# Down-projection of a hybrid layer: sample columns in two transfers, samples and operand work behind the tile, another order of sums

## The chip, the cores and the metric

One core of a Trainium2 chip runs the whole program. The metric is the device time of one execution in microseconds. Engines and queues are named as in the profile: TensorE is PE (its weight loads PEld), VectorE is DVE, ScalarE is ACT, GpSimd is POOL, SyncE is SP. Every DMA of the stage concerned is issued by SP.

## The reference

One layer over 1024 prompt rows and 32 sample rows: a mixer (a state-space group and an attention group side by side), then a gated feed-forward. Width 1024, feed-forward width 2816. The change touches the last product:

```python
    x = x + jnp.concatenate([y_ssd, o], axis=-1) @ w_out
    f = rmsnorm(x, norm_ffn_g)
    x = x + (jax.nn.silu(f @ w_gate) * (f @ w_up)) @ w_down
```

It is taken for the prompt rows (1024 x 2816 by 2816 x 1024) and for the sample rows.

## The kernel before, in words

**Gate and up** come first (matmuls at L970, added up by DVE at L978). Their result, the activations of 22 blocks of 128 feed-forward columns, is formed block pair by block pair. For the prompt, `keep` (L1007) splits each of seven combinations per pair into a rounded part (ACT cast, L1012) and a remainder (DVE, L1013) and writes both to DRAM, `act_d` (L1015, 256 KB a write). It uses two sets of pieces of the tile `sc` in turn, so a combination waits for the writes of the one before the last. For the sample rows, a small slice per block goes to `asm_d` (L1003).

**Down** is lines 1036 to 1229. There are NP = 11 pairs `n` of weight blocks. A product of 2 x 2 blocks is made with seven products instead of eight; each product is three matmuls per pair (rounded by rounded, rounded by remainder, remainder by rounded). The work goes in six chunks, and in each over four token tiles `tp`:

```python
    chunks_ = [(0, 1)] + [(n, 2) for n in range(1, NP, 2)]
    tiles_ = [(n0, r, tp) for n0, r in chunks_ for tp in range(4)]
```

Chunk 0 has one pair (tiles of 21 matmuls), the others have two (42). `down_tile` (L1145) makes the seven products of a tile in banks `ps_z` and adds them into `Z` in SBUF (copies by ACT L1171 and DVE L1173 in chunk 0, additions by DVE L1160 later). The last chunk also combines and stores.

For each pair, `prep_down` (L1060) does four things: the **sample product** of 16 small matmuls (L1064) that wants the sample columns `asm` and both weight blocks `raw`; its addition to `x2s` (DVE, L1067); the **splits** of the operands into a rounded part (ACT, L1077) and a remainder (DVE, L1078); and the **sums** on POOL (L1082, L1083, L1085, L1086). The operands are W (one block, unsummed), X (the second `raw`), V (the first `raw` after two sums) and U (after two more). X, V and U take the next of nine slots in turn: five are pairs of tiles `whi`, `wlo`; four lie in `sd` (tag "lo"), in the memory of the `sc` pieces that `keep` wrote from.

Weight blocks come by `load_raw` (L1051, 512 KB each, two per pair), activations by `load_act` (L1045, 896 KB per pair and tile) into five slots: four in `fA` and `at5`. At the start of Down, SP issues `raw` of pairs 1 and 2, then `asm` in one transfer of 352 KB (L1127). A scheduler merges the order in which the code is written with what is ready; the built order below is its result. Per queue and engine, instructions run in that order.

Of the kernel before, what the change touches and what calls it, by code (L numbers as in the profile page):

```python
# [7 lines left out]
F32 = mybir.dt.float32  # L8
# [4 lines left out]
ALU = mybir.AluOpType  # L13
AX = mybir.AxisListType

P = 128
# [4 lines left out]
NS = 32  # L21
# [6 lines left out]
NF = 22  # L28
NP = NF // 2
# [14 lines left out]
def build(tc, a):  # L44
    nc = tc.nc
# [26 lines left out]
    def nm(s):  # L72
        cnt[0] += 1
        return f"{s}_{cnt[0]}"
# [43 lines left out]
    asm_d = dr.tile([P, NF, NS], F32, name="asm_d")  # L118
# [677 lines left out]
    units, _ = pipelined([unit(i, pair) for pair in range(4) for i in (ORDER if pair < 3 else LAST)] + [None, None])  # L796
# [108 lines left out]
    def wide():  # L905
        return pv.tile([P, 1024], F32, tag="w", bufs=4, name=nm("ps_w"))
# [7 lines left out]
    T2, T1, T3, B22, T4 = (tq.tile([P, 2, 4, H], F32R, name=n) for n in ("T2", "T1", "T3", "B22", "T4"))  # L914
# [13 lines left out]
    B11 = fA[:, :, 0:4, :]  # L928
    B21 = fA[:, :, 4:8, :]
# [102 lines left out]
    ats, raws, bops = {}, {}, {}  # L1032
# [4 lines left out]
    asm0 = mixS[:, 0:2, :]  # L1037
# [10 lines left out]
    def load_raw(n, pl, bufs):  # L1048
        raws[n] = [pl.tile([P, 1024], F32, tag="raw", bufs=bufs, name=nm("raw")) for _ in range(2)]
        for k in range(2):  # L1050
            nc.sync.dma_start(raws[n][k], a["wd"][2 * n + k])  # L1051

    def next_slot():
        k = b_turn[0]
        b_turn[0] += 1
        if k < 5:
            b_slots.append([wp.tile([P, 1024], F32R, tag=tag, bufs=5, name=nm(tag)) for tag in ("whi", "wlo")])
        return b_slots[k % 9]

    def prep_down(n, pb, act):  # L1060

        for k in range(2):
            for g in range(4):
                nc.tensor.matmul(pb[32 * g:32 * g + 32, 0:256], lhsT=act[:, k, :],  # L1064
                                 rhs=raws[n][k][:, g * 256:(g + 1) * 256], start=(k == 0), stop=(k == 1),
                                 tile_position=(0, 32 * g))
        nc.vector.tensor_tensor(x2s, pb[:, 0:256], x2s, op=ALU.add)  # L1067
        r1, r2 = raws.pop(n)
        b11, b12, b21, b22 = r1[:, 0:512], r1[:, 512:1024], r2[:, 0:512], r2[:, 512:1024]
        if n < 3:  # L1070
            c_slots.append(wp.tile([P, 1024], F32, tag="raw", bufs=3, name=nm("raw")))
        c = c_slots[n % 3].bitcast(F32R)
        W = [c[:, 0:512], c[:, 512:1024]]
        X, V, U = (next_slot() for _ in range(3))

        def split(t, src):
            nc.scalar.copy(out=t[0], in_=src)  # L1077
            nc.vector.tensor_tensor(t[1], src, t[0], op=ALU.subtract)  # L1078

        split(W, b11)  # L1080
        split(X, r2)
        nc.gpsimd.tensor_tensor(b12, b22, b12, op=ALU.subtract)  # L1082
        nc.gpsimd.tensor_tensor(b11, b12, b11, op=ALU.add)  # L1083
        split(V, r1)
        nc.gpsimd.tensor_tensor(b22, b22, b11, op=ALU.subtract)  # L1085
        nc.gpsimd.tensor_tensor(b21, b21, b11, op=ALU.subtract)  # L1086
        split(U, r2)
        op = lambda t, c: [x[:, c:c + 512] for x in t]
        bops[n] = dict(B11=op(W, 0), B21=op(X, 0), B22=op(X, 512), T2=op(V, 0), T3=op(V, 512), T4=op(U, 0), T1=op(U, 512))

    chunks_ = [(0, 1)] + [(n, 2) for n in range(1, NP, 2)]
    tiles_ = [(n0, r, tp) for n0, r in chunks_ for tp in range(4)]
# [3 lines left out]
    for k, (w, n) in enumerate(work):  # L1096
        end = k + 1 == len(work)
        cur = ops
        if not end:
            ops = prep(*work[k + 1])  # L1100
            use = use_up(n) if w else use_gate
        else:
            load_raw(0, wp, 3)
            nc.sync.dma_start(asm0, asm_d[:, 0:2])
            prep_down(0, wide(), asm0)

            def use(b, h, then=use_up(n)):
                if b == 0 and h == 0:
                    for m in range(4):
                        load_act(tiles_[m])  # L1110
                then(b, h)
        quad(cur, acts if w else gates, use)
        if w:
            keep_acts(n)
# [6 lines left out]
    pd = pool("pd", side="right")  # L1121
    pz = pool("pz", space=PSUM)
    Z = [pd.tile([P, 4, 512], F32, name=f"Z{k}") for k in range(7)]
    load_raw(1, pd, 4)
    load_raw(2, pd, 4)
    asm = pd.tile([P, NF, NS], F32, name="asm")
    nc.sync.dma_start(asm, asm_d)  # L1127
    at_slots.append(pd.tile([P, 7 * 2 * P], F32R, name="at5"))
    at_turn[0] = 4
    sd = hp.tile([P, KB * NT], F32R, tag="lo", name="sd")  # L1130
# [5 lines left out]
    def bank1():  # L1136
        return pz.tile([P, 512], F32, tag="z", bufs=8, name=nm("ps_z"))

    def residual(tp, rows, cols, z):
        x = pd.tile([P, 512], F32, tag="res", bufs=1, name=nm("res"))  # L1140
        r0 = 512 * rows + tp * P
        nc.sync.dma_start(x, xb_d[r0:r0 + P, 512 * cols:512 * cols + 512])
        nc.gpsimd.tensor_tensor(z, x, z, op=ALU.add)

    def down_tile(m):  # L1145
        n0, r, tp = tiles_[m]
        first, late, last = n0 == 0, n0 == NP - 4, n0 == NP - 2
        at = ats.pop(tiles_[m])
        z = [None] + [Z[i][:, tp, :] for i in range(7)]

        def product(q, name):
            pb = bank1()
            terms = [(k, x, y) for k in range(r) for x, y in ((0, 0), (0, 1), (1, 0))]
            for i, (k, x, y) in enumerate(terms):
                nc.tensor.matmul(pb, lhsT=at[k][:, q, x, :], rhs=bops[n0 + k][name][y], start=(i == 0),  # L1155
                                 stop=(i == len(terms) - 1))
            return pb

        def add(o, x, y, eng=nc.vector):
            eng.tensor_tensor(o, x, y, op=ALU.add)  # L1160

        def store(v, rows, cols):
            nc.sync.dma_start(a["o_yp"][(4 * rows + tp) * P:(4 * rows + tp + 1) * P, 512 * cols:512 * cols + 512], v)

        order = ((1, A11, "B11"), (6, S2, "T2"), (2, A12, "B21"), (5, S1, "T1"), (7, S3, "T3"), (3, S4, "B22"),
                 (4, A22, "T4"))
        if not last:
            for i, q, name in order:
                pb = product(q, name)
                if first and i in (1, 2, 5, 4):  # L1170
                    nc.scalar.copy(out=z[i], in_=pb)  # L1171
                elif first:
                    nc.vector.tensor_copy(z[i], pb)  # L1173
                else:
                    add(z[i], pb, z[i])
            if n0 in (3, 5):

                for i, rows, cols in ((2, 0, 0), (3, 0, 1), (4, 1, 0))[(0 if n0 == 3 else 2):(2 if n0 == 3 else 3)]:
                    residual(tp, rows, cols, z[i])
            if late:  # L1180

                add(z[6], z[1], z[6])
                add(z[2], z[1], z[2], nc.gpsimd)
                add(z[5], z[6], z[5])
                add(z[1], z[6], z[7])
                add(z[3], z[5], z[3], nc.gpsimd)
                add(z[7], z[5], z[7])
                add(z[4], z[1], z[4], nc.gpsimd)
                residual(tp, 1, 1, z[7])
            return  # L1190
        eng = nc.vector if tp == 3 else nc.gpsimd
        nc.scalar.copy(out=z[1], in_=product(A11, "B11"))
        add(z[6], product(S2, "T2"), z[1])
        add(z[2], z[1], z[2], eng)
        add(z[2], product(A12, "B21"), z[2])
        store(z[2], 0, 0)
        add(z[5], product(S1, "T1"), z[6])
        p7 = product(S3, "T3")
        add(z[7], z[5], z[7], eng)
        add(z[3], z[5], z[3], eng)  # L1200
        add(z[1], p7, z[6])
        add(z[7], p7, z[7])
        store(z[7], 1, 1)
        add(z[4], z[1], z[4], eng)
        add(z[3], product(S4, "B22"), z[3])
        store(z[3], 0, 1)
        add(z[4], product(A22, "T4"), z[4])
        store(z[4], 1, 0)

    def prep_next(n):  # L1210
        if n < NP:
            prep_down(n, bank1(), asm[:, 2 * n:2 * n + 2])
            if n + 2 < NP:
                load_raw(n + 2, pd, 4)

    for m in range(len(tiles_)):
        n0, r, tp = tiles_[m]

        if tp == (0 if r == 1 else 2):
            prep_next(n0 + r)  # L1220
        elif tp == 2:
            prep_next(n0 + r + 1)
        down_tile(m)
        if r == 2 and tp == 3:
            prep_next(n0 + r + 1)
        for k in {0: (4,), 2: (5,)}.get(m, (m + 2,) if m > 3 else ()):
            if k < len(tiles_):
                load_act(tiles_[k])
# [76 lines left out]
```

## Time and profile before

| | us |
|---|---|
| median of 3 runs | 1378.44 (1378.04 to 1383.52) |
| the profiled execution | 1378.53 |
| its span, first to last instruction | 1376.8 |
| TensorE busy | 1289.9 (94%) |
| DVE busy | 905.5 (66%) |
| POOL busy | 613.3 (45%) |
| ACT busy | 503.0 (37%) |

The span counts from the first to the last instruction; an execution's time is a little longer. Busy shares are means over stages of different kinds. The stage concerned begins at about 1122 us of the span, so it is the last 255 us. Times in the rows below count from the span's start.

### The profile page before, as it was taken

The numbers are of one execution on the slowest core, as the hardware profiler recorded it, in microseconds if no ns is written. First come the engines' busy times: TensorE is split into PE (matmuls) and PEld (weight loads), VectorE is DVE, ScalarE is ACT, GpSimd is POOL, SyncE is SP. The second block draws the span as 40 slices with busy tenths as digits, with TensorE's granted clock in tenths as the row PEclk, the third lists the DMA queues.
The fourth block names the chain that finished last, engine by engine and source line by source line (L and its number), as shares of the span: only waits on it lengthen the run. The fifth ranks groups of instructions, "written<-read, shape, count | busy, mean of one in ns | idle before, by whom it ended". The sixth has DMA issues, their size and how long they took to land.

```text
span 1376.8 us, 23827 instructions
## 1 busy us (share of the span) xinstructions
PE 1289.9 (94%) x9260; PEld 1175.1 (85%) x9260; DVE 905.5 (66%) x1271; ACT 503.0 (37%) x865; POOL 613.3 (45%) x507
## 2 busy tenths in 40 slices
PE   5999999977998999898799999999999969999988
PEld 4999999967887688687799999999999957787766
DVE  5346437785748555765867667767667766666886
ACT  7245332322346543653533334333333424111110
POOL 7142248987636100301343445444354433255485
PEclk9999999979999999999799999999999988999999
DMA  7265342445386976755134445544545576567755
GB/s 268 75 209 155 95 168 60 150 152 172 116 254 194 342 244 213 227 164 171 51 115 134 139 139 170 154 125 125 152 133 162 155 266 223 206 240 288 251 198 178
DMA packets 201456, 242.02 MB, mean 176 GB/s; under 512 B 25696, under 2 KB 162976, under 8 KB 201344
## 3 DMA queue, kind: packets, MB, share of 16 engines
q1 hardware_dynamic: 201344, 240.51, 54.2%
q8 instruction: 73, 1.20, 0.4%
q14 instruction: 39, 0.32, 0.1%
HBM read 149.47 MB, written 90.99 MB: 175 GB/s over the span
## 4 chain that ended last, share of the span: by engine, by line
PE 65%; issue 10%; POOL 8%; DVE 7%; DMA 6%; ACT 2%; SPq 0%; POOLq 0%; ACTq 0%; DVEq 0%
PE ps_w L970 33%; PE ps_z L1155 5%; PE ps_mm L153 4%; PE ps_mm L154 4%; PE ps_mm L155 4%; DVE Z L1160 2%; PE ps_mm L160 2%; PE ps_mm L162 2%; PE ps_mm L161 2%; DMA res<-xb_d 2%; PE ps_mm L734 2%; PE ps_t L717 1%; PE ps_s L695 1%; DMA mix_d<-ot 1%; POOL dm L541 1%
## 5 line engine op out<-in xcount | busy, mean ns | idle before, releaser
L970 PE MATMUL ps_w<-T,whi 128*128 128x264 f32 x1408 | 231.0, 286 | 4.9 <-ACT T L918 4.9
L970 PEld LDWEIGHTS ps_w<-T,whi 128*128 128x128 f32 x1408 | 196.7, 191 | 5.4 <-ACT T L918 5.4
L978 DVE TENSOR_TENSOR sc<-sc,ps_w 128x528 f32<-128x528 f32 x154 | 105.5, 698 | 79.8 <-PE ps_w L970 77.7
L153 PE MATMUL ps_mm<-whi,hT_hi 128*128 128x256 f32 (+1 forms) x512 | 149.2, 291 | 4.8 <-ACT hT_hi L227 3.2
L155 PE MATMUL ps_mm<-whi,hT_lo 128*128 128x256 f32 (+1 forms) x512 | 148.6, 290 | 0.4 <-DVE hT_lo L228 0.4
L154 PE MATMUL ps_mm<-wlo,hT_hi 128*128 128x256 f32 (+1 forms) x512 | 148.5, 290 | 0.0
L970 PE MATMUL ps_w<-T,wlo 128*128 128x264 f32 x704 | 144.8, 288 | 0.0
L139 POOL TENSOR_TENSOR wlo<-raw,whi 128x1024 fp32r<-128x1024 f32 (+1 forms) x32 | 80.8, 2532 | 134.9 <-ACT whi L138 133.5
L946 ACT CAST whi<-raw 128x1024 fp32r<-128x1024 f32 x88 | 82.7, 941 | 101.3 <-PE ps_w L970 86.3
L970 PE MATMUL ps_w<-fA,whi 128*128 128x264 f32 x704 | 117.0, 289 | 0.0
L1160 DVE TENSOR_TENSOR Z<-ps_z,Z 128x512 f32<-128x512 f32 x140 | 92.3, 685 | 33.9 <-PE ps_z L1155 30.2
L947 DVE TENSOR_TENSOR wlo<-raw,whi 128x1024 fp32r<-128x1024 f32 x88 | 107.5, 1223 | 6.1 <-ACT whi L946 3.7
L1013 DVE TENSOR_TENSOR sc<-sc 128x512 fp32r<-128x512 f32 x77 | 75.6, 993 | 54.2 <-DMA act_d<-sc 30.3
L970 PEld LDWEIGHTS ps_w<-T,wlo 128*128 128x128 f32 x704 | 110.3, 191 | 0.0
L153 PEld LDWEIGHTS ps_mm<-whi,hT_hi 128*128 128x128 f32 x512 | 99.5, 194 | 6.9 <-ACT hT_hi L227 3.6
L1155 PE MATMUL ps_z<-whi,fA 128*128 128x512 f32 x276 | 99.6, 400 | 3.2 <-DVE Z L1160 1.7
L155 PEld LDWEIGHTS ps_mm<-whi,hT_lo 128*128 128x128 f32 x512 | 99.6, 195 | 1.8 <-DVE hT_lo L228 0.8
L970 PEld LDWEIGHTS ps_w<-fA,whi 128*128 128x128 f32 x704 | 100.6, 193 | 0.4 <-PE ps_w L1064 0.4
L154 PEld LDWEIGHTS ps_mm<-wlo,hT_hi 128*128 128x128 f32 x512 | 99.3, 194 | 0.3
L1012 ACT CAST sc<-sc 128x512 fp32r<-128x512 f32 x77 | 46.7, 621 | 117.5 <-DVE sc L1002 69.8
L954 POOL TENSOR_TENSOR raw<-raw,raw 128x512 f32<-128x512 f32 x22 | 37.1, 1687 | 90.8 <-DVE wlo L947 90.8
L970 PE MATMUL ps_w<-fA,wlo 128*128 128x264 f32 x352 | 72.4, 288 | 0.0
(282 smaller groups left out, 3105.5 us busy)
## 6 DMA issues: line engine op xcount, KB each, us to landing
act_d<-sc SPq DMA_DIRECT2D x154, 256.0 KB, 2.9
fA<-act_d SPq DMA_DIRECT2D x36, 896.0 KB, 6.0
raw<-in_wgu_dram SPq DMA_DIRECT2D x44, 512.0 KB, 3.6
raw<-in_wd_dram SPq DMA_DIRECT2D x22, 512.0 KB, 4.1
x<-in_xp_dram SPq DMA_DIRECT2D x16, 512.0 KB, 6.6
q<-qst_d SPq DMA_DIRECT2D x32, 256.0 KB, 4.9
mx<-mix_d SPq DMA_DIRECT2D x16, 512.0 KB, 4.6
raw<-in_wq_dram SPq DMA_DIRECT2D x14, 512.0 KB, 4.8
```

The source lines that it names most:

```text
L139: (eng or nc.gpsimd).tensor_tensor(lo, raw, hi, op=ALU.subtract)
L153: nc.tensor.matmul(ps_, lhsT=lh, rhs=rh, start=start, stop=False)
L154: nc.tensor.matmul(ps_, lhsT=lh, rhs=rl, start=False, stop=False)
L155: nc.tensor.matmul(ps_, lhsT=ll, rhs=rh, start=False, stop=stop)
L946: nc.scalar.copy(out=t[0][:, 0:w], in_=src)
L947: nc.vector.tensor_tensor(t[1][:, 0:w], src, t[0][:, 0:w], op=ALU.subtract)
L970: nc.tensor.matmul(out[:, h, :], lhsT=A[x][:, kb, :], rhs=B[:, y, kb, h * Q:(h + 1) * Q], start=(n == 0), stop=(n == len(terms) - 1))
L978: add = lambda o, x, y: nc.vector.tensor_tensor(o, x, y, op=ALU.add)
L1012: nc.scalar.copy(out=hi.bitcast(F32R), in_=src)
L1013: nc.vector.tensor_tensor(lo.bitcast(F32R), src, hi, op=ALU.subtract)
L1155: nc.tensor.matmul(pb, lhsT=at[k][:, q, x, :], rhs=bops[n0 + k][name][y], start=(i == 0), stop=(i == len(terms) - 1))
L1160: eng.tensor_tensor(o, x, y, op=ALU.add)
```

## The change

`prep_down` falls into `sample_down` (sample product and its addition), `prep_first` (split of W, first two sums) and `prep_rest` (the other splits and sums). The operands are made in the order V, X, U instead of X, V, U, and the sums for U are written into the first `raw` of the pair instead of the second. `asm` is loaded in two transfers: 20 of 22 columns behind `raw` of pair 1, the last two behind tile 2. For each tile, `down_tile` comes first and the next pairs' samples and operands behind it. In chunks of two pairs, the second pair's sample moves from behind tile 3 to behind tile 2. The late sums of the chunk before the last go into `combine`, called one tile later.

```diff
--- before.py
+++ after.py
@@ -1057,7 +1057,7 @@
             b_slots.append([wp.tile([P, 1024], F32R, tag=tag, bufs=5, name=nm(tag)) for tag in ("whi", "wlo")])
         return b_slots[k % 9]
 
-    def prep_down(n, pb, act):
+    def sample_down(n, pb, act):
 
         for k in range(2):
             for g in range(4):
@@ -1065,28 +1065,34 @@
                                  rhs=raws[n][k][:, g * 256:(g + 1) * 256], start=(k == 0), stop=(k == 1),
                                  tile_position=(0, 32 * g))
         nc.vector.tensor_tensor(x2s, pb[:, 0:256], x2s, op=ALU.add)
-        r1, r2 = raws.pop(n)
-        b11, b12, b21, b22 = r1[:, 0:512], r1[:, 512:1024], r2[:, 0:512], r2[:, 512:1024]
+
+    def split_to(t, src):
+        nc.scalar.copy(out=t[0], in_=src)
+        nc.vector.tensor_tensor(t[1], src, t[0], op=ALU.subtract)
+
+    def prep_first(n):
+
+        r1, r2 = raws[n]
         if n < 3:
             c_slots.append(wp.tile([P, 1024], F32, tag="raw", bufs=3, name=nm("raw")))
         c = c_slots[n % 3].bitcast(F32R)
         W = [c[:, 0:512], c[:, 512:1024]]
-        X, V, U = (next_slot() for _ in range(3))
-
-        def split(t, src):
-            nc.scalar.copy(out=t[0], in_=src)
-            nc.vector.tensor_tensor(t[1], src, t[0], op=ALU.subtract)
-
-        split(W, b11)
-        split(X, r2)
-        nc.gpsimd.tensor_tensor(b12, b22, b12, op=ALU.subtract)
-        nc.gpsimd.tensor_tensor(b11, b12, b11, op=ALU.add)
-        split(V, r1)
-        nc.gpsimd.tensor_tensor(b22, b22, b11, op=ALU.subtract)
-        nc.gpsimd.tensor_tensor(b21, b21, b11, op=ALU.subtract)
-        split(U, r2)
+        split_to(W, r1[:, 0:512])
+        nc.gpsimd.tensor_tensor(r1[:, 512:1024], r2[:, 512:1024], r1[:, 512:1024], op=ALU.subtract)
+        nc.gpsimd.tensor_tensor(r1[:, 0:512], r1[:, 512:1024], r1[:, 0:512], op=ALU.add)
+        bops[n] = dict(B11=W)
+
+    def prep_rest(n):
+        r1, r2 = raws.pop(n)
+        V, X, U = (next_slot() for _ in range(3))
+        split_to(V, r1)
+        split_to(X, r2)
+
+        nc.gpsimd.tensor_tensor(r1[:, 512:1024], r2[:, 512:1024], r1[:, 0:512], op=ALU.subtract)
+        nc.gpsimd.tensor_tensor(r1[:, 0:512], r2[:, 0:512], r1[:, 0:512], op=ALU.subtract)
+        split_to(U, r1)
         op = lambda t, c: [x[:, c:c + 512] for x in t]
-        bops[n] = dict(B11=op(W, 0), B21=op(X, 0), B22=op(X, 512), T2=op(V, 0), T3=op(V, 512), T4=op(U, 0), T1=op(U, 512))
+        bops[n].update(B21=op(X, 0), B22=op(X, 512), T2=op(V, 0), T3=op(V, 512), T4=op(U, 0), T1=op(U, 512))
 
     chunks_ = [(0, 1)] + [(n, 2) for n in range(1, NP, 2)]
     tiles_ = [(n0, r, tp) for n0, r in chunks_ for tp in range(4)]
@@ -1102,7 +1108,9 @@
         else:
             load_raw(0, wp, 3)
             nc.sync.dma_start(asm0, asm_d[:, 0:2])
-            prep_down(0, wide(), asm0)
+            sample_down(0, wide(), asm0)
+            prep_first(0)
+            prep_rest(0)
 
             def use(b, h, then=use_up(n)):
                 if b == 0 and h == 0:
@@ -1121,10 +1129,10 @@
     pd = pool("pd", side="right")
     pz = pool("pz", space=PSUM)
     Z = [pd.tile([P, 4, 512], F32, name=f"Z{k}") for k in range(7)]
+    asm = pd.tile([P, NF, NS], F32, name="asm")
     load_raw(1, pd, 4)
+    nc.sync.dma_start(asm[:, 0:NF - 2], asm_d[:, 0:NF - 2])
     load_raw(2, pd, 4)
-    asm = pd.tile([P, NF, NS], F32, name="asm")
-    nc.sync.dma_start(asm, asm_d)
     at_slots.append(pd.tile([P, 7 * 2 * P], F32R, name="at5"))
     at_turn[0] = 4
     sd = hp.tile([P, KB * NT], F32R, tag="lo", name="sd")
@@ -1142,9 +1150,17 @@
         nc.sync.dma_start(x, xb_d[r0:r0 + P, 512 * cols:512 * cols + 512])
         nc.gpsimd.tensor_tensor(z, x, z, op=ALU.add)
 
+    def combine(tp):
+
+        z = [None] + [Z[i][:, tp, :] for i in range(7)]
+        for o, x, y, eng in ((6, 1, 6, nc.vector), (2, 1, 2, nc.gpsimd), (5, 6, 5, nc.vector), (1, 6, 7, nc.vector),
+                             (3, 5, 3, nc.gpsimd), (7, 5, 7, nc.vector), (4, 1, 4, nc.gpsimd)):
+            eng.tensor_tensor(z[o], z[x], z[y], op=ALU.add)
+        residual(tp, 1, 1, z[7])
+
     def down_tile(m):
         n0, r, tp = tiles_[m]
-        first, late, last = n0 == 0, n0 == NP - 4, n0 == NP - 2
+        first, last = n0 == 0, n0 == NP - 2
         at = ats.pop(tiles_[m])
         z = [None] + [Z[i][:, tp, :] for i in range(7)]
 
@@ -1177,16 +1193,6 @@
 
                 for i, rows, cols in ((2, 0, 0), (3, 0, 1), (4, 1, 0))[(0 if n0 == 3 else 2):(2 if n0 == 3 else 3)]:
                     residual(tp, rows, cols, z[i])
-            if late:
-
-                add(z[6], z[1], z[6])
-                add(z[2], z[1], z[2], nc.gpsimd)
-                add(z[5], z[6], z[5])
-                add(z[1], z[6], z[7])
-                add(z[3], z[5], z[3], nc.gpsimd)
-                add(z[7], z[5], z[7])
-                add(z[4], z[1], z[4], nc.gpsimd)
-                residual(tp, 1, 1, z[7])
             return
         eng = nc.vector if tp == 3 else nc.gpsimd
         nc.scalar.copy(out=z[1], in_=product(A11, "B11"))
@@ -1207,22 +1213,26 @@
         add(z[4], product(A22, "T4"), z[4])
         store(z[4], 1, 0)
 
-    def prep_next(n):
-        if n < NP:
-            prep_down(n, bank1(), asm[:, 2 * n:2 * n + 2])
-            if n + 2 < NP:
-                load_raw(n + 2, pd, 4)
-
     for m in range(len(tiles_)):
         n0, r, tp = tiles_[m]
-
-        if tp == (0 if r == 1 else 2):
-            prep_next(n0 + r)
-        elif tp == 2:
-            prep_next(n0 + r + 1)
         down_tile(m)
-        if r == 2 and tp == 3:
-            prep_next(n0 + r + 1)
+
+        for n, sample, rest in ((n0 + r, *((0, 0) if r == 1 else (1, 1))), (n0 + r + 1, *((1, 1) if r == 1 else (2, 3)))):
+            if n >= NP:
+                continue
+            if tp == sample:
+                sample_down(n, bank1(), asm[:, 2 * n:2 * n + 2])
+            if tp == rest:
+                prep_first(n)
+                prep_rest(n)
+                if n + 2 < NP:
+                    load_raw(n + 2, pd, 4)
+        if n0 == NP - 4 and tp > 0:
+            combine(tp - 1)
+        elif n0 == NP - 2 and tp == 0:
+            combine(3)
+        if m == 2:
+            nc.sync.dma_start(asm[:, NF - 2:NF], asm_d[:, NF - 2:NF])
         for k in {0: (4,), 2: (5,)}.get(m, (m + 2,) if m > 3 else ()):
             if k < len(tiles_):
                 load_act(tiles_[k])
```

Three places in the built order (before: L1064, L1155, L1077; after: L1064, L1171, L1070).

TensorE at the start of Down, before. `ps_w` belongs to the last gate/up product, `ps_z` to Down.

```order
L970 MATMUL ps_w_1749_12247<-T4_7218,whi_1724_11845 128x264 x4
L970 MATMUL ps_w_1749_12247<-T4_7218,wlo_1725_11846 128x264 x2
L1064 MATMUL ps_z_1758_12338<-raw_1750_12322,asm_12330 32x256 x4
L1064 MATMUL ps_z_1758_12338<-raw_1751_12323,asm_12330 32x256 x4
L1155 MATMUL ps_z_1766_12369<-raw_1736_12061,fA_4995 128x512 x3
L1155 MATMUL ps_z_1767_12374<-whi_1739_12064,fA_4995 128x512
L1155 MATMUL ps_z_1767_12374<-wlo_1740_12065,fA_4995 128x512
L1155 MATMUL ps_z_1767_12374<-whi_1739_12064,fA_4995 128x512
```

The same place after. `raw_1736` and `whi_1737` to `whi_1741` are operands of pair 0.

```order
L970 MATMUL ps_w_1749_12247<-T4_7218,whi_1724_11845 128x264 x4
L970 MATMUL ps_w_1749_12247<-T4_7218,wlo_1725_11846 128x264 x2
L1171 MATMUL ps_z_1758_12338<-raw_1736_12061,fA_4995 128x512 x3
L1171 MATMUL ps_z_1759_12343<-whi_1737_12066,fA_4995 128x512
L1171 MATMUL ps_z_1759_12343<-wlo_1738_12067,fA_4995 128x512
...
L1171 MATMUL ps_z_1764_12368<-wlo_1742_12071,fA_4995 128x512
L1171 MATMUL ps_z_1764_12368<-whi_1741_12070,fA_4995 128x512
L1064 MATMUL ps_z_1765_12373<-raw_1750_12323,asm_12322 32x256 x4
L1064 MATMUL ps_z_1765_12373<-raw_1751_12324,asm_12322 32x256 x4
L1171 MATMUL ps_z_1773_12406<-raw_1736_12061,fA_4995 128x512 x3
```

The first sample product stood ahead of tile 0 (its first product is `ps_z_1766` before, `ps_z_1758` after) and now stands behind its 21 matmuls.

SP, before, from the first `raw` of pair 1 to the first activations of chunk 1 in `fA`. `act_d` are the writes of kept activations, `at5` and `fA` loads of activations.

```order
L1051 DMA raw_1750_12322<-in_wd_dram 128x1024
L1051 DMA raw_1751_12323<-in_wd_dram 128x1024
L1051 DMA raw_1752_12326<-in_wd_dram 128x1024
L1051 DMA raw_1753_12327<-in_wd_dram 128x1024
L1003 DMA asm_d_83<-sc_7230 128x16
L1015 DMA act_d_82<-sc_7230 512x1x128 x4
L1045 DMA at5_12332<-act_d_82 128x1792
L1142 DMA res_1839_12880<-xb_d_81 128x512
L1127 DMA asm_12330<-asm_d_83 128x704
L1015 DMA act_d_82<-sc_7230 512x1x128 x6
L1051 DMA raw_1764_12365<-in_wd_dram 128x1024
L1045 DMA fA_4995<-act_d_82 128x1792
```

SP, after, from the same `raw`.

```order
L1051 DMA raw_1750_12323<-in_wd_dram 128x1024
L1051 DMA raw_1751_12324<-in_wd_dram 128x1024
L1134 DMA asm_12322<-asm_d_83 128x640
L1051 DMA raw_1752_12328<-in_wd_dram 128x1024
L1003 DMA asm_d_83<-sc_7230 128x16
L1015 DMA act_d_82<-sc_7230 512x1x128
L1051 DMA raw_1753_12329<-in_wd_dram 128x1024
...
L1045 DMA fA_4995<-act_d_82 128x1792
L1235 DMA asm_12322<-asm_d_83 128x64
L1015 DMA act_d_82<-sc_7230 512x1x128 x2
L1045 DMA fA_4995<-act_d_82 128x1792
L1015 DMA act_d_82<-sc_7230 512x1x128 x2
L1051 DMA raw_1771_12400<-in_wd_dram 128x1024
L1045 DMA fA_4995<-act_d_82 128x1792
L1015 DMA act_d_82<-sc_7230 512x1x128 x2
```

The columns `asm` moved from behind four `raw`, `act_d`, `at5` and `res` to third place, and three loads into `fA` and one `raw` moved ahead of the last two `act_d`. Left out at the dots: three `act_d`, `at5` and a residual row.

ACT in chunk 0, before. `sc` is `keep`'s, `sd` the slots in its memory.

```order
L1012 CAST sc_7230<-sc_7230 128x512 x3
L1171 COPY Z0_12315<-ps_z_1766_12369 128x512
L1077 CAST whi_1756_12336<-raw_1750_12322 128x1024
L1077 CAST sd_12333<-raw_1753_12327 128x1024
L1171 COPY Z1_12316<-ps_z_1768_12379 128x512
L1171 COPY Z4_12319<-ps_z_1769_12384 128x512
L1077 CAST sd_12333<-raw_1751_12323 128x1024
```

ACT after, at the first cast into `sd`.

```order
L1012 CAST sc_7230<-sc_7230 128x512
L1187 COPY Z0_12315<-ps_z_1791_12506 128x512
L1187 COPY Z1_12316<-ps_z_1793_12516 128x512
L1187 COPY Z4_12319<-ps_z_1794_12521 128x512
L1187 COPY Z3_12318<-ps_z_1797_12536 128x512
L1070 CAST raw_1736_12061<-raw_1771_12400 128x512
L1070 CAST sd_12333<-raw_1750_12323 128x1024
L1070 CAST sd_12333<-raw_1752_12328 128x1024
L1070 CAST sd_12333<-raw_1753_12329 128x1024
L1070 CAST whi_1739_12068<-raw_1772_12401 128x1024
L1070 CAST sd_12333<-raw_1752_12328 128x1024
```

The first cast into `sd` made X of pair 2 and stood right behind tile 0's first copy; it now makes U of pair 1 and stands behind the whole of chunk 0. Behind it in ACT's order stand X of pair 3 (`raw_1772`) and, after that, U of pair 2.

## Rows read from the trace of the kernel before

**Rows 1.** The page's part 1: busy us (share of the span) xinstructions
```profile
PE 1289.9 (94%) x9260; PEld 1175.1 (85%) x9260; DVE 905.5 (66%) x1271; ACT 503.0 (37%) x865; POOL 613.3 (45%) x507
```

**Rows 2.** TensorE's waits, 1122 to 1163: us in total, times, longest
```profile
PE ps_z L1064 <- DMA asm<-asm_d: 15.8, 1, 15.8
```

**Rows 3.** The same list, 1326 to 1346
```profile
PE ps_z L1155 <- DVE Z L1160: 1.7, 1, 1.7
PE ps_z L1155 <- ACT whi L1077: 1.4, 1, 1.4
PE ps_z L1155 <- DVE wlo L1078: 0.9, 2, 0.6
```

**Rows 4.** Stretches: us, busy PE PEld DVE ACT POOL, PEclk, DMA share, GB/s
```profile
1122.00:1124.00 2.00, 0.40 (x4) 0.18 (x2) 1.53 (x2) 0.00 (x0) 1.92 (x2) 1.00 0.79 181
1124.00:1140.00 16.00, 1.82 (x16) 0.68 (x16) 7.17 (x8) 5.27 (x8) 3.90 (x4) 0.61 1.02 342
1128.00:1144.00 16.00, 5.82 (x25) 3.84 (x26) 6.08 (x9) 4.83 (x8) 4.52 (x5) 0.50 0.90 292
1145.00:1147.00 2.00, 2.00 (x11) 1.65 (x10) 2.00 (x2) 1.87 (x3) 0.99 (x1) 1.00 0.04 4
1300.00:1320.00 20.00, 20.00 (x100) 15.79 (x99) 19.97 (x23) 1.67 (x2) 17.00 (x11) 1.00 0.63 218
1336.00:1339.00 3.00, 3.00 (x9) 2.12 (x8) 1.26 (x3) 0.00 (x0) 3.00 (x3) 0.50 1.00 407
```

**Rows 5.** TensorE's timeline: start, length, line, tiles, shapes, count [idle before <-releaser]
```profile
1121.99 0.41 PE L970 MATMUL ps_w<-T,wlo 128*128 128x264 f32 x2
1138.18 1.94 PE L1064 MATMUL ps_z<-raw,asm 128*32 128x256 f32 x16 [15.79 <-DMA asm<-asm_d]
...
1141.50 0.63 PE L1155 MATMUL ps_z<-whi,fA 128*128 128x512 f32 x1
1141.92 0.63 PE L1155 MATMUL ps_z<-wlo,fA 128*128 128x512 f32 x1
```

**Rows 6.** The same of SP: its DMA issues
```profile
1121.76 1.95 SPq L1051 DMA_DIRECT2D raw<-in_wd_dram  x4
...
1131.27 0.38 SPq L1127 DMA_DIRECT2D asm<-asm_d  x1
1132.28 9.45 SPq L1015 DMA_DIRECT2D act_d<-sc  x6
```

**Rows 7.** DMA issues, 1100 to 1175: count, KB each, median us to landing
```profile
raw<-in_wd_dram SPq DMA_DIRECT2D x8, 512.0 KB, 4.9
...
asm<-asm_d SPq DMA_DIRECT2D x1, 352.0 KB, 6.7
```

**Rows 8.** TensorE's timeline: the first two tiles of chunk 1 start
```profile
1162.53 0.86 PE L1155 MATMUL ps_z<-raw,at 128*128 128x512 f32 x3
...
1172.29 1.52 PE L1155 MATMUL ps_z<-raw,fA 128*128 128x512 f32 x6
```

**Rows 9.** ACT's timeline
```profile
1129.46 0.62 ACT L1077 CAST raw<-raw 128x512 fp32r<-128x512 f32 x1 [0.85 <-DMA raw<-in_wd_dram]
...
1143.87 1.05 ACT L1077 CAST sd<-raw 128x1024 fp32r<-128x1024 f32 x1 [0.47 <-DMA act_d<-sc]
```

**Rows 10.** Groups of instructions, 1163 to 1300: busy us, mean ns | idle before
```profile
L1078 DVE TENSOR_TENSOR wlo<-raw,whi 128x1024 fp32r<-128x1024 f32 x11 | 15.7, 1423 | 7.7 <-ACT whi L1077 7.6
...
L1086 POOL TENSOR_TENSOR raw<-raw,raw 128x512 f32<-128x512 f32 x6 | 12.7, 2123 | 0.0
...
L1085 POOL TENSOR_TENSOR raw<-raw,raw 128x512 f32<-128x512 f32 x6 | 7.8, 1298 | 0.5
```

**Rows 11.** Timelines of TensorE and ACT at the boundary before chunk 4
```profile
1286.21 0.97 PE L1155 MATMUL ps_z<-raw,fA 128*128 128x512 f32 x3
...
1294.42 1.05 ACT L1077 CAST sd<-raw 128x1024 fp32r<-128x1024 f32 x1 [2.56 <-POOL raw L1086]
```

**Rows 12.** TensorE's waits, 1163 to 1326
```profile
PE ps_z L1155 <- DMA fA<-act_d: 0.2, 1, 0.2
```

## Prediction

> **What bounds the kernel now.** First the page's busy table: TensorE is busy for 94% of the 1376.8 us span [rows 1], so time is to be had only where it stands still or runs at half clock. Next the list of its waits by stretch. From 1122 to 1163 there is one wait, 15.8 us of the first sample product for the sample columns, `asm` [rows 2]. From 1326 to 1346, around the last chunk's start, there are three, 4.0 us together [rows 3]. Between them, 1163 to 1326, it waits for 0.2 us [rows 12].
>
> The timeline shows the first hole from inside [rows 5]: the last gate/up matmuls start at 1121.99 and end at 1122.4, the sample product starts at 1138.18, and the tile's own matmuls follow at once. Their operands are ready; they merely stand behind the sample in TensorE's order. The hole costs more than its length: the granted clock over 1128 to 1144 is 0.50 (1.2 GHz), from 1145 it is 1.00 (2.4 GHz) [rows 4]. It fell while TensorE was idle and came back some 6 us into the new work.
>
> Why is `asm` late? On SP its issue, at 1131.27, comes 9.5 us behind the first of the four `raw` [rows 6], with four `act_d`, `at5` and a residual row between them, and then needs 6.7 us to land [rows 7]. The transfers are busy all that while: 342 GB/s from 1124 to 1140 at a DMA share of 1.02 [rows 4]. So it stands in a queue that is full, and its place in SP's order sets when it lands.
>
> **The change, part by part.** The number of engine instructions stays; one DMA is added. What changes is order.
>
> **1. Front of Down: a lead of 17 us by the end of chunk 0.** Tile 0 may start at 1122.4. A tile of 42 matmuls takes 1172.29 - 1162.53 = 9.76 us at full clock [rows 8], so one of 21 takes 4.9: tile 0 ends at 1127.3. Then comes sample 1, which wants both `raw` of pair 1 and the first 20 columns. In the new SP order these are transfers one, two and three. Before, the third transfer of this place, a `raw` of 512 KB, had landed when ACT cast it at 1129.46 [rows 9]; the 320 KB of columns in its place should land about 0.6 us earlier, near 1128.8. TensorE waits 1.5 us, then runs the sample (1.94 us at half clock [rows 5], so 0.97), tile 1, sample 2, tile 2, tile 3: 1128.8 + 2 x 0.97 + 3 x 4.9 = 1145.4. Chunk 0 ended at 1162.53 before [rows 8]; the lead is 17 us. Cross-check: 15.8 of wait, less 1.5 of new wait, plus the clock. From 1138.18 to 1162.53 before are 24.35 us for 4 x 4.9 + 2 x 0.97 = 21.5 us of full-clock work, so the clock had cost 2.8, and 15.8 - 1.5 + 2.8 = 17.1. I take 17.
>
> **2. What is late next: the operand U of pair 1, minus 8.0 us.** In chunk 1, TensorE has twelve matmuls on operands in ordinary buffers (W and the first halves of V and X), 12 x 0.232 = 2.8 us, to 1148.2. The thirteenth needs U of pair 1, which lies in `sd`. That buffer lies over the `sc` pieces from which the kept activations are written, so the ACT cast into it must wait until the last `act_d` write has landed. Before, that cast began at 1143.87, held up for 0.47 us by just that [rows 9], and nobody noticed, TensorE being late itself.
>
> Now TensorE arrives early, and the writes leave later. In the new SP order three loads of activations (896 KB each, free as soon as tiles 0 to 2 are done) and one `raw` (512 KB) have moved ahead of the last two `act_d` writes: 3.28 MB. Two ways to price it. Everything from the first `raw` to the last write is 9.53 MB (five `raw` 2.62, columns 0.36, ten `act_d` 2.62, `at5` and three more loads 3.67, a residual row 0.26); at 342 GB/s that is 27.9 us. The 181 GB/s over 1122 to 1124 [rows 4] are as if the transfers began at 1122.9, so 1150.8. Or 3.28 MB, 9.6 us, on top of 1143.87: 1153.5. Before, the last of the six `act_d` issues ended at 1141.73 [rows 6] and that write had landed 2.1 us later, so little stood in front of it any more, and the second way counts too much. I take the first and add those 2.1 us: 1152.9. The cast of 1.05 us follows [rows 9]: 1154.0. TensorE waits 5.8 us.
>
> A wait of that length brings the clock down, by the first hole. The price lies between the 2.8 us above and the smaller second dip, where TensorE ran at 0.50 for 3 us after waits of 1.67 and 0.64 us [rows 3, 4], costing 1.5. I take 2.2. Then the lead is 17 - 5.8 - 2.2 = 9.0 us. Behind it ACT casts X of pair 3 before U of pair 2, and that `raw` is issued only after the subtraction into `sd`, about 1155.5; with 4.9 us to landing [rows 7] and two casts, U of pair 2 is there at 1162.5. TensorE comes to it 32 matmuls after 1154.0, 7.4 us plus the clock's 2.2, at 1163.6: covered by a microsecond, no more.
>
> The Trainium skill, "DMA: Bandwidth & Descriptors", Specifications, gives 435 GB/s as the fabric's ceiling and some 358 GB/s as one core's share of HBM. The measured 342 is close to the second; by the first, as an estimate, 9.53 MB would be through 6 us earlier, part 2 would cost nothing, and the sum would be 1361.5. No stretch in these rows holds such a rate for the 28 us that this would want.
>
> **3. Operands in the order V, X, U.** V's subtraction on DVE now stands between POOL's two pairs of sums, since POOL writes U over `r1`. That puts a cast of 1.05 and a subtraction of 1.42 on U's path [rows 9, 10]. At the chunk's start TensorE also wants U earlier, after 34 matmuls of the tile (7.9 us) instead of 48 (11.1 us), by the built order. Against that the second pair's sample is a whole tile earlier, 9.8 us, so POOL no longer waits for it at the boundary. Before, at the boundary at 1286.21, the last U cast ended at 1295.47 [rows 11], 9.3 us into the tile, in time for 11.1. Now V's buffer comes free 17 matmuls before the boundary (3.9 us); cast 1.05, subtraction 1.4, two sums of 1.3 to 2.1, cast 1.05 give 2.2 to 3.8 us into the tile, against 7.9. So 0, with 4 us in hand. If this cover is gone, each of four boundaries pays.
>
> **4. Late sums one tile later, and the last chunk.** The scheduler put them at nearly the same places. DVE is busy 19.97 of 20 us in 1300 to 1320 [rows 4], so the end of that stretch stays DVE's. Of the 4.0 us of waits [rows 3] plus 1.5 of clock the V-first order might take some or add to them; bounds plus 5 and minus 2, I take 0.
>
> **Sum:** 9.0 us, all of it from parts 1 and 2. The profiled execution took 1378.53 us, 1.7 over its span and 0.1 over the median of 1378.44. 1378.5 - 9.0 = **1369.5 us**.
>
> **Rivals.** About 0.5% (6.9 us) is what a measurement of this kernel can tell from no change; under 1371.5 is faster, above 1385.3 slower.
>
> *The lead is kept.* If the last writes land by 1147 (or the built order lets TensorE find other work), part 2 is nought: 17 us, 1361.5; with all of the late waits gone too, 1356. For it: DMA reached 407 GB/s in 1336 to 1339 [rows 4]. Against: 342 over the stretch concerned. Chance 0.22.
>
> *Most of it is given back.* The writes land at 1157.6 (9.53 MB at 292 GB/s, the mean from 1128 to 1144 [rows 4], and the 2.1), the `raw` behind them holds up U of pair 2 as well, and the clock stays low between the two waits: 32 matmuls at the 0.42 us that half clock shows [rows 5] instead of 0.232 are 6 us more. The wait is then 10.5 us and the lead 17 - 10.5 - 6 = 0.5 us: 1378. Chance 0.19.
>
> *Slower: the V-to-U chain.* Its place is the four boundaries between pairs of chunks. DVE and POOL slow each other there: POOL's two U sums are the same shape, yet 1298 ns (L1085) and 2123 ns (L1086) [rows 10], the second beside a DVE subtraction. If V's subtraction stands behind additions on DVE, as in 1300 to 1320, U comes late. It decides once U is 4 us later than worked out, and outweighs 9.0 + 6.9 us only from 8 us per boundary. At 10 us it gives 4 x 6 - 9.0 = 15 slower: 1393.5. Against: only 0.2 us of waits in 1163 to 1326 [rows 12], where no chain of this kind was late by as much. Chance 0.04. The Trainium skill, "SBUF — State Buffer", Who interferes with whom, says that a DVE instruction with two SBUF inputs and a GpSimd one that reads SBUF exclude each other for a whole instruction, which would make it a rule, not an accident; the 2123 agrees.
>
> *The columns do not come early.* If the small rows of the first part are as slow as before, 6.7 us from an issue at 1123, they land at 1130: 1.2 us less gain, inside the forecast.
>
> **The numbers.** Forecast 0.55 (1365 to 1374: the wait for `sd` 2 us either way, the clock 0.7, the last chunk 2), lead kept 0.22, given back 0.19, slower 0.04. Of the forecast's own spread 0.07 falls above 1371.5. Faster 0.48 + 0.22 = 0.70, same 0.07 + 0.19 = 0.26, slower 0.04. The range from 1359.5 to 1377 takes in most of the first rival and the better half of the second.
>
> **What would show it.** In the new profile: tile 0 right behind gate/up at 1122.4; a wait of 1 to 3 us for `asm`; chunk 0 over at 1145 to 1147; one wait of 3 to 8 us on ACT's cast into `sd`, itself released by the `act_d` writes; a dip of the clock behind it; no waits worth 1 us from 1170 to 1290. It is wrong if the `sd` wait is missing, if TensorE waits at each boundary for U, or if the first hole is still there.

## The result, and the profile after

| | before | after |
|---|---|---|
| median (lowest to highest) | 1380.98 us (1378.04 to 1385.31, 4 runs) | 1362.95 us (1359.27 to 1365.81, 4 runs) |
| the profiled execution | 1378.53 us | 1365.81 us |
| its span | 1376.8 us | 1364.1 us |
| Down alone: end of the last gate/up matmul to the span's end | 254.4 us | 241.0 us |

The ratio is 0.9865, 95% interval 0.9825 to 0.9906: 18 us faster by the medians, 12.7 by the two profiled executions. Forecast were 9.0 us and 1369.5, range 1359.5 to 1377. The last line of the table is used throughout: what lies ahead of Down is the same code in all kernels here, but for the operands of pair 0, and yet Down begins between 1120.1 and 1125.9 us of the span in the ten profiles of this study. Down's own length leaves that out.

TensorE's waits in the changed kernel, first 1118 to 1163, which answers to [rows 2]; none is listed for 1163 to 1300 [rows 12]:

```profile
PE ps_z L1171 <- ACT sd L1070: 6.9, 1, 6.9
PE ps_z L1064 <- DMA asm<-asm_d: 2.1, 1, 2.1
```

and from 1300 to the end, where before there were three of 4.0 us together [rows 3]:

```profile
PE ps_z L1171 <- ACT sd L1070: 0.9, 1, 0.9
```

The 15.8 us for the columns have become 2.1; a new wait of 6.9 us stands in chunk 1, where the forecast put one of 5.8; and the last chunk has lost most of its waits, which was not forecast. TensorE's timeline at the front (columns as in [rows 5]):

```profile
1122.68 0.41 PE L970 MATMUL ps_w<-T,wlo 128*128 128x264 f32 x2
1122.93 0.86 PE L1171 MATMUL ps_z<-raw,fA 128*128 128x512 f32 x3
...
1129.95 1.07 PE L1064 MATMUL ps_z<-raw,asm 128*32 128x256 f32 x16 [2.06 <-DMA asm<-asm_d]
...
1146.97 0.86 PE L1171 MATMUL ps_z<-raw,at 128*128 128x512 f32 x3
...
1149.53 0.39 PE L1171 MATMUL ps_z<-whi,at 128*128 128x512 f32 x1
1156.82 0.80 PE L1171 MATMUL ps_z<-sd,at 128*128 128x512 f32 x1 [6.89 <-ACT sd L1070]
```

Tile 0 runs straight behind gate/up, chunk 1 starts at 1146.97 instead of 1162.53 [rows 8], and twelve matmuls later TensorE stands still for the first operand in `sd`. ACT's timeline says what that cast waited for (compare 1143.87 in [rows 9]), and SP's when the writes left:

```profile
1155.72 2.94 ACT L1070 CAST sd<-raw 128x1024 fp32r<-128x1024 f32 x3 [3.81 <-DMA act_d<-sc]
```

```profile
1123.51 0.42 SPq L1134 DMA_DIRECT2D asm<-asm_d  x1
...
1144.23 0.34 SPq L1051 DMA_DIRECT2D raw<-in_wd_dram  x1
1144.66 0.39 SPq L1045 DMA_DIRECT2D fA<-act_d  x1
1145.15 1.39 SPq L1015 DMA_DIRECT2D act_d<-sc  x2
```

The last two `act_d` left at 1145.15 and 1145.8, behind a `raw` and an activation load, and 9.5 us later they had landed. The stretches show the clock (columns as in [rows 4]):

```profile
1124.00:1140.00 16.00, 13.94 (x83) 9.68 (x82) 12.61 (x15) 10.20 (x18) 10.01 (x7) 1.00 1.02 363
...
1155.00:1160.00 5.00, 3.18 (x8) 2.54 (x9) 3.20 (x3) 2.94 (x3) 0.70 (x1) 0.50 0.22 56
1160.00:1165.00 5.00, 5.00 (x22) 4.09 (x21) 2.04 (x3) 2.00 (x2) 2.72 (x2) 0.96 0.37 121
```

Up to the new wait it is at full rate (2.4 GHz); behind it, it is at half rate (1.2 GHz) to 1160 and a little beyond.

**Where the time came from.** The starts of equal tiles give the lead of the changed kernel. Chunk 1: 1162.53 - 1146.97 = 15.6 us. Chunk 2: 1203.41 - 1196.76 = 6.7. Chunk 3: 1244.46 - 1237.77 = 6.7. Chunk 4: 1286.21 - 1278.53 = 7.7. Chunk 5: 1327.28 - 1319.54 = 7.7. End: 12.7. So 6.7 us come from the front (15.6, less 6.9 of wait and 2.0 of clock), 1.0 from chunk 3 and 5.0 from the last chunk. These are times of the span; in this profile Down begins 0.7 us later than before (the last gate/up matmul ends at 1123.1 instead of 1122.4), and counted from there every lead is 0.7 larger.

The lines on which the last term rests are the starts of the last chunk, before and in the change:

```profile
1327.28 1.65 PE L1155 MATMUL ps_z<-raw,fA 128*128 128x512 f32 x6
```

```profile
1319.54 1.53 PE L1171 MATMUL ps_z<-raw,fA 128*128 128x512 f32 x6
```

From there to the span's end it is 49.5 us before and 44.6 in the change. This length of the last chunk is used below as well.

### The profile page after: what moved, and what is told of

It is laid out like the page before. It is cut to its first block, busy times and chain, and to the rows that moved or that the text cites. A ratio compares the mean times of both kernels' runs of the same rounds, so it can differ in the third digit from the quotient of the medians.

```text
span 1364.1 us, 23795 instructions
## 1 busy us (share of the span) xinstructions
PE 1286.8 (94%) x9260; PEld 1172.2 (86%) x9260; DVE 904.8 (66%) x1271; ACT 502.6 (37%) x865; POOL 616.6 (45%) x507
## 4 chain that ended last, share of the span: by engine, by line
PE 66%; POOL 7%; DVE 7%; DMA 6%; issue 6%; ACT 1%; SPq 1%; DVEq 0%; ACTq 0%; POOLq 0%
PE ps_w L970 33%; PE ps_z L1171 11%; PE ps_mm L153 3%; PE ps_mm L154 3%; PE ps_mm L155 3%; PE ps_mm L162 2%; PE ps_mm L160 2%; PE ps_mm L161 2%; PE ps_mm L734 1%; PE ps_t L717 1%; POOL dm L541 1%; PE ps_s L695 1%; DMA qst_d<-st 1%; POOL rs_r L146 1%; DVE Z L1176 1%
## 5 line engine op out<-in xcount | busy, mean ns | idle before, releaser
L1171 PE MATMUL ps_z<-whi,fA 128*128 128x512 f32 x276 | 97.5, 391 | 0.0
```

## The experiments

In all of them "Down" is the length defined above, and the change itself has 241.0 us there in its first profile and 237.7 in its second.

**The columns' place alone.** The kernel before with the columns in two transfers; everything else in the old order.

```diff
-    load_raw(1, pd, 4)
-    load_raw(2, pd, 4)
     asm = pd.tile([P, NF, NS], F32, name="asm")
-    nc.sync.dma_start(asm, asm_d)
+    load_raw(1, pd, 4)
+    nc.sync.dma_start(asm[:, 0:NF - 2], asm_d[:, 0:NF - 2])
+    load_raw(2, pd, 4)
...
+        if m == 2:
+            nc.sync.dma_start(asm[:, NF - 2:NF], asm_d[:, NF - 2:NF])
```

> The kernel before with one part of the change: the sample columns in two transfers, the first behind the raw of pair 1; the sample still stands ahead of tile 0. Theory (place in the queue sets when the columns land): they land near 1129.5, TensorE waits 7 us there instead of 15.8, chunk 0 ends near 1153 instead of 1162.5, and 9 to 10 us of that are kept, as the writes of kept activations are not pushed back: 1369 to 1372. Rival (the columns need what they need, the order of the engines is what gains): wait of 12 us or more, under 4 us gained.

Measured: 1372.23 us (ratio 0.9934, 0.9915 to 0.9953), Down 246.3. TensorE's waits, at the front and in the last chunk:

```profile
PE ps_z L1064 <- DMA asm<-asm_d: 7.7, 1, 7.7
```

```profile
PE ps_z L1155 <- ACT whi L1077: 2.3, 1, 2.3
PE ps_z L1155 <- DVE Z L1160: 2.0, 2, 1.6
PE ps_z L1155 <- DVE wlo L1078: 0.9, 2, 0.6
```

The wait halves, chunk 1 starts 30.6 us behind gate/up instead of 40.1, so 9.5 us of lead, and there is no wait for `sd`. 8.1 us of it are left at the end: the last chunk's waits are a little longer than before (5.2 us, and 51.0 us for the chunk). The theory held; the time is 0.2 us above its 1369 to 1372. The place in the queue is worth half of the hole by itself.

**The order alone.** The changed kernel with the columns in one transfer behind `raw` of pair 2.

```diff
     load_raw(1, pd, 4)
-    nc.sync.dma_start(asm[:, 0:NF - 2], asm_d[:, 0:NF - 2])
     load_raw(2, pd, 4)
+    nc.sync.dma_start(asm, asm_d)
...
-        if m == 2:
-            nc.sync.dma_start(asm[:, NF - 2:NF], asm_d[:, NF - 2:NF])
```

> The changed kernel, but the columns in one transfer behind the raw of pair 2, as before. Theory: tile 0 runs at once, then TensorE waits about 10 us for the columns at 1127 to 1138; the front keeps some 5 us of its lead, there is no wait for sd, and the last chunk keeps its gain of 5 us: 1367 to 1371, 4 to 7 us slower than the change. Rival (the tile ahead of the sample is what gains, the columns' place is not): within 2 us of the change.

Measured: 1370.99 us (ratio 0.9927, 0.9902 to 0.9951), Down 247.0.

```profile
PE ps_z L1064 <- DMA asm<-asm_d: 14.7, 1, 14.7
```

The wait is 14.7 us, not the 10 of the expectation: with tile 0 out of the way, its freed buffer lets a load of activations go out ahead of the columns. They are issued 11.0 us behind gate/up instead of 8.9 and are there after 19.5 us instead of 15.8. Against the change the kernel is 8.0 us slower by the medians, more than the 4 to 7 expected. Chunk 1 starts 38.5 us behind gate/up instead of 40.1, a lead of 1.6, and the other 5.8 of the 7.4 us gained come behind it. So neither part fills the front's hole without the other: early columns alone leave 7.7 us, the order alone 14.7, both 2.1 and what follows from them.

**The order of the operands.**

```diff
-        V, X, U = (next_slot() for _ in range(3))
-        split_to(V, r1)
-        split_to(X, r2)
+        X, V, U = (next_slot() for _ in range(3))
+        split_to(X, r2)
+        split_to(V, r1)
...
-        nc.gpsimd.tensor_tensor(r1[:, 512:1024], r2[:, 512:1024], r1[:, 0:512], op=ALU.subtract)
-        nc.gpsimd.tensor_tensor(r1[:, 0:512], r2[:, 0:512], r1[:, 0:512], op=ALU.subtract)
-        split_to(U, r1)
+        nc.gpsimd.tensor_tensor(r2[:, 512:1024], r2[:, 512:1024], r1[:, 0:512], op=ALU.subtract)
+        nc.gpsimd.tensor_tensor(r2[:, 0:512], r2[:, 0:512], r1[:, 0:512], op=ALU.subtract)
+        split_to(U, r2)
```

> The changed kernel with the operands in the old order X, V, U and U's sums in the second raw again. If V first is what took the waits out of the last chunk: 3 to 4 us of waits and a clock dip come back at its start, 4 to 5 us slower than the change, front unchanged. Rival (late sums or samples one tile earlier took them out): last chunk as in the change, within 1.5 us of it.

Measured: 1364.63 us (ratio 0.9883, 0.9846 to 0.9920), Down 244.8. Waits in the last chunk:

```profile
PE ps_z L1171 <- ACT whi L1070: 0.7, 1, 0.7
PE ps_z L1171 <- ACT sd L1070: 0.6, 1, 0.6
```

1.3 us, and the last chunk takes 44.5 us as in the change, so V first is not what took the waits out there. What V first is worth at all stays open: the medians lie 1.7 us apart with intervals that overlap, while this profile's Down is 3.8 to 7.1 us longer, from a clock dip in chunk 0 behind a wait of 2.6 us and from a wait of 1.8 us for activations in chunk 3 (45.0 us long instead of 40.8), which may be this execution's.

**The late sums, and the second pair's sample.** Two kernels, each with one of them put back:

```diff
-        if n0 == NP - 4 and tp > 0:
-            combine(tp - 1)
-        elif n0 == NP - 2 and tp == 0:
-            combine(3)
+        if n0 == NP - 4:
+            combine(tp)
```

> The changed kernel with the late sums of each tile straight behind that tile, as before, not one tile later. If the sums' place took the waits out of the last chunk: 3 to 4 us of waits and a clock dip come back at its start, 4 to 5 us slower than the change. Rival (the earlier sample of the second pair took them out): waits under 1.5 us as in the change, within 1 us of it.

```diff
-        for n, sample, rest in ((n0 + r, *((0, 0) if r == 1 else (1, 1))), (n0 + r + 1, *((1, 1) if r == 1 else (2, 3)))):
+        for n, sample, rest in ((n0 + r, *((0, 0) if r == 1 else (1, 1))), (n0 + r + 1, *((1, 1) if r == 1 else (3, 3)))):
```

> The changed kernel with the sample of a chunk's second pair behind tile 3 again instead of behind tile 2. If the earlier sample took the waits out of the last chunk: POOL's sums start 9.8 us later at each boundary, U comes late by some us, 3 to 4 us of waits come back at the last chunk and perhaps less at the others, 3 to 6 us slower than the change. Rival (the late sums' place did it): within 1 us of the change.

Measured: sums put back 1360.46 us (0.9860, 0.9823 to 0.9897), Down 238.0, last chunk 44.6: no difference that can be told. Sample put back 1369.41 us (0.9926, 0.9904 to 0.9948), Down 246.9, beside 1362.81 for the change in the same comparison: 6.6 us slower by the medians (the intervals just touch), 5.9 to 9.2 us by Down. Its last chunk takes 50.4 us, 5.8 more than in the change; what goes beyond that lies at the front, where a wait of 2.8 us and a dip of the clock stand in this profile. Where its last chunk starts, and the waits in it:

```profile
1316.81 1.65 PE L1171 MATMUL ps_z<-raw,fA 128*128 128x512 f32 x6
```

```profile
PE ps_z L1171 <- DVE wlo L1071: 2.0, 2, 1.7
PE ps_z L1171 <- ACT whi L1070: 1.4, 1, 1.4
```

Waits are back, 3.4 us. How the sample does it is seen on POOL and ACT around the start of the last chunk. First POOL's first sum for the last pair, in the kernel before, in the change and with the sample put back, from the timeline of each:

```profile
1335.74 1.73 POOL L1082 TENSOR_TENSOR raw<-raw,raw 128x512 f32<-128x512 f32 x1
```

```profile
1313.70 2.28 POOL L1081 TENSOR_TENSOR raw<-raw,raw 128x512 f32<-128x512 f32 x1
```

```profile
1325.41 1.74 POOL L1081 TENSOR_TENSOR raw<-raw,raw 128x512 f32<-128x512 f32 x1
```

Then the cast that hangs on the second sum, before, in the change and with the sample put back:

```profile
1341.22 1.04 ACT L1077 CAST whi<-raw 128x1024 fp32r<-128x1024 f32 x1 [11.66 <-POOL raw L1083]
```

```profile
1320.65 2.00 ACT L1070 CAST whi<-raw 128x1024 fp32r<-128x1024 f32 x2 [7.02 <-POOL raw L1082]
```

```profile
1330.12 1.04 ACT L1070 CAST whi<-raw 128x1024 fp32r<-128x1024 f32 x1 [10.21 <-POOL raw L1082]
```

The sums write into the `raw` that the sample product still reads. Counted from the start of the last chunk, the first sum starts 8.5 us behind it, 5.8 us ahead of it and 8.6 us behind it: with the earlier sample POOL gets to it before its queue fills with additions for `Z`. The cast comes 13.9, 1.1 and 13.3 us into the chunk. In both kernels with the late sample TensorE waits 1.4 us for it and 0.3 us for the remainder made from it.

That is 1.7 of the 4.0 us of waits before. The other 2.3 us [rows 3] are 1.7 for an addition to `Z` on DVE and 0.6 for a remainder whose cast was over at 1325.4 while DVE came to it at 1333.4. With the sample put back, the other 1.7 us are for a remainder of the pair ahead (pair 9), whose last sum on POOL is late there (1315.67, 1.1 us ahead of the chunk, against 1310.31, 9.2 us ahead, in the change):

```profile
1315.67 1.73 POOL L1092 TENSOR_TENSOR raw<-raw,raw 128x512 f32<-128x512 f32 x1
```

```profile
1310.31 1.72 POOL L1092 TENSOR_TENSOR raw<-raw,raw 128x512 f32<-128x512 f32 x1
```

So it is shown that the last chunk is 5.8 us longer without the earlier sample, and by which chain for half of the waits. How the sample's place acts on the other half is not shown; the order of the additions on POOL and DVE moves with it.

**The wait on `sd`.** The change, with U of pair 1 and V and X of pair 2 in the three buffers that pair 0 leaves; only U of pair 2 lies in `sd` in chunk 1. The splits concerned move behind tile 3, where those buffers are free, and with them the loads of `raw` for pairs 3 and 4.

```diff
-        if k < 5:
+        if k < 3:
...
-        return b_slots[k % 9]
+        return b_slots[([0, 1, 2] + [3, 4, 0, 1, 2, 5, 6, 7, 8] * 4)[k]]
...
-                prep_rest(n)
-                if n + 2 < NP:
+                if n == 1:
+                    prep_vx(n)
+                    prep_sums(n)
+                elif n > 2:
+                    prep_rest(n)
+                if n > 2 and n + 2 < NP:
                     load_raw(n + 2, pd, 4)
+        if m == 3:
+            prep_u(1)
+            prep_rest(2)
+            load_raw(3, pd, 4)
+            load_raw(4, pd, 4)
```

(`prep_vx`, `prep_sums` and `prep_u` are the three parts of `prep_rest`)

> The changed kernel with one thing more: U of pair 1 and V and X of pair 2 take the three operand buffers of pair 0, free at the end of tile 3, and only U of pair 2 lies in sd in chunk 1. Theory (the 6.9 us wait in chunk 1 is the aliasing of sd with the kept activations' writes): the wait goes or shrinks below 1.5 us, no clock dip, 7 to 9 us faster than the change, profiled 1357 to 1359. Rival (DMA is so full that something else is late there, raw of pair 3 or the activations): a wait of 4 us or more under another name, at most 3 us faster.

Measured: 1355.12 us (ratio 0.9811, 0.9774 to 0.9848), Down 232.1. All of TensorE's waits from 1115 to 1170, and the stretch in which the change stood still:

```profile
PE ps_z L1064 <- DMA asm<-asm_d: 1.0, 1, 1.0
PE ps_z L1184 <- DVE x2s L1067: 0.6, 1, 0.6
```

```profile
1145.00:1160.00 15.00, 15.00 (x67) 12.29 (x66) 13.74 (x16) 5.04 (x6) 3.45 (x2) 1.00 0.93 331
```

The wait is gone, the clock stays at 1.00, and the transfers are as full as ever (331 GB/s) without anything being late. The rival falls. Nor is it that the writes land earlier: the last two `act_d` leave at 1142.7 and 1143.7 and need 9.1 to 9.4 us, so they land near 1152.8, 8 us into chunk 1 (it starts at 1145.00), and the first cast into `sd` begins behind them:

```profile
1153.16 1.05 ACT L1070 CAST sd<-raw 128x1024 fp32r<-128x1024 f32 x1 [3.32 <-DMA fA<-act_d]
```

That it is the buffer on which the wait hung is thus shown. Then both kernels once more side by side:

> The changed kernel once more, as the measure for the runs beside it: 1359 to 1366, a wait of 6 to 8 us on sd in chunk 1.

> The changed kernel with the buffers of pair 0 for U of pair 1 and V and X of pair 2, once more beside the change: 1354 to 1356, 7 to 10 us faster than the change.

Measured: the change 1362.81 us (0.9873, 0.9838 to 0.9907), Down 237.7; with the buffers 1356.79 us (0.9828, 0.9788 to 0.9868), Down 232.2. The change's wait and clock in this profile:

```profile
PE ps_z L1171 <- ACT sd L1070: 4.3, 1, 4.3
```

```profile
1150.00:1155.00 5.00, 3.72 (x10) 2.89 (x11) 3.50 (x3) 2.94 (x3) 1.23 (x1) 0.67 0.47 162
1155.00:1160.00 5.00, 5.00 (x23) 4.11 (x22) 2.34 (x3) 2.00 (x2) 2.21 (x2) 0.99 0.35 124
```

So the wait on `sd` varies, 6.9 and 4.3 us in two executions of one kernel (expected were 6 to 8 in the second), and 3.3, 4.6 and 3.6 us in the kernels with the operands, the late sums and the sample put back; the two profiles without the wait have Down within 0.1 us of each other. The other buffers give 6 to 8 us by the medians (the two intervals of the second comparison overlap), 5.5 to 8.9 by Down; the 6.0 of the second comparison are below the 7 to 10 expected. This is the fastest kernel of the study, faster than both that it started from.

## Why the prediction was right, point by point

The direction, the range and the two largest steps held; the size was half of what the medians show. That the median lies in the range is in part luck: 1362.95 is below the 1365 to 1374 of the forecast proper and near the 1361.5 of the rival *the lead is kept*, for whose sake the range reached down to 1359.5, and that rival's condition did not come true. By the steps:

- **Part 1, the front.** Forecast: a new wait of 1.5 us and a lead of 17 at chunk 1. Measured 2.06 and 15.6, or 16.3 from Down's beginning; in the second profile of the change, counted so, 1.3 and 17.0. The columns landed in third place; the two experiments on their place and on the order show that both are needed.
- **Part 2, what is late next.** Forecast: a wait of 5.8 us for U of pair 1 in `sd`, and 2.2 us of clock. Measured 6.9 and 2.0 in one profile, 4.3 and 1.9 in the other; taking U out of `sd` removed it. The lead left was forecast at 9.0 and is 6.7 (7.4 from Down's beginning; 10.7 in the second profile). The rate over 1124 to 1140 was 363 GB/s, not 342, and yet the cast found the last `act_d` landed only at 1155.7, where 1152.9 had been worked out, 0.7 of it from Down's later beginning. Two things that the sum of bytes did not see stand in the rows. The rate fell behind 1140, to 319 and 283 GB/s:

```profile
1140.00:1145.00 5.00, 5.00 (x24) 4.14 (x23) 5.00 (x8) 3.01 (x6) 4.20 (x3) 1.00 0.98 319
1145.00:1150.00 5.00, 4.92 (x22) 3.69 (x20) 2.19 (x4) 1.21 (x3) 0.00 (x0) 1.00 0.98 283
```

And the last issues were held up by other engines: the `raw` of pair 3 went out only when POOL had finished U's sums of pair 1 (1144.20), and the last write's own remainder came from DVE only at 1145.12, behind four copies into `Z`:

```profile
1142.91 1.29 POOL L1092 TENSOR_TENSOR raw<-raw,raw 128x512 f32<-128x512 f32 x1
```

```profile
1142.05 2.47 DVE L1189 COPY Z<-ps_z 128x512 f32<-128x512 f32 x4
1144.44 0.68 DVE L1013 TENSOR_TENSOR sc<-sc 128x512 fp32r<-128x512 f32 x1
```

That write left at 1145.8, so the `raw` ahead of it can have cost it 0.7 us at most. How the rest divides stays open.
- **Part 3, V, X, U.** Forecast 0 with 4 us in hand. No wait from 1163 to 1300, so nothing of the slower rival's chain was seen. What the order itself gives is open.
- **Part 4, the last chunk, is the step that failed.** It said that "the end of that stretch stays DVE's" and took 0 within plus 5 and minus 2. It is plus 5.0, the upper bound, in both profiles of the change. The full DVE of [rows 4] was read as the limit. But 1.7 of the 4.0 us hung on a chain from sample to POOL's sums to cast, and the earlier sample, which part 3 counted as mere cover at the boundaries, shortened just that chain; the 2.3 us that did hang on DVE went too, in a way that the runs do not show. Putting the sample back made the last chunk 5.8 us longer; putting the late sums or the operand order back did not.
- **A term left out:** 1.0 us in chunk 3, which took 41.75 us before and 40.76 in the change. It belongs to the order and not to the columns' place: the kernel before with early columns has 41.64 us there, the changed kernel with late columns 40.77. What in the order gives it stays open.
- **The rivals.** "The lead is kept" needs no wait on `sd`; the change doesn't reach it, the kernel with other buffers does, at 1355.1 where the rival with the late waits gone was priced at 1356. "Most is given back" and "slower" did not come.

The 5.3 us by which 18 exceeds the profiled 12.7 are the choice of executions: the profile of before is near its lowest run, that of the change is its slowest. The second profile of the change, 16.7 us shorter in Down than before, is nearer to the medians; there the shorter wait on `sd` left 10.7 us of the front's lead, and chunk 3 and the last chunk gave 1.0 and 5.0 as in the first.

## What to carry to other kernels

An engine that runs in order waits for its first late operand even if the work behind it is ready: put a small product that wants a late transfer behind work that is ready, and the transfer ahead in its queue, both at once. When such a hole is filled, look at once for the next thing that was hidden by it; here it was a buffer in the memory of another stage's outgoing writes, and giving the first operands needed another buffer was worth as much again as was left of the gain at the front. And an operand that POOL overwrites in place is held by its last reader: a reader that can go earlier frees the whole chain behind it, which a list of busy shares doesn't show.

## What the runs showed of the hardware that was not expected

The granted clock fell behind one short wait and not behind another of about the same length. Behind 2.06 us in the change the sample product took 1.07 us, at full rate (2.4 GHz), while behind 2.58 us with the operands in the old order the same 16 matmuls took 1.93 us, at half rate (1.2 GHz), and behind 2.83 us with the sample put back 1.77 us:

```profile
1129.80 1.93 PE L1064 MATMUL ps_z<-raw,asm 128*32 128x256 f32 x16 [2.58 <-DMA asm<-asm_d]
```

Nor did a longer wait cost more of the clock. Chunk 1 takes 40.9 us in both profiles without a wait there. Behind the wait of 6.9 us it took 49.8, behind 4.3 us 47.1 and behind 3.3 us (old operand order) 47.3, so besides the wait itself 2.0, 1.9 and 3.1 us were lost. So the price of a short wait is not its length: 2 to 3 us can hang on it, and single profiles differ by that.
